# First-half token sums beside the second sample group's cross-attention, three units in the late tail, and low parts of the sums on VectorE

## The chip, the cores and the metric

The kernel runs on one core of a Trainium2 chip, as one program and one launch. The metric is device time in microseconds (us); the time of a kernel is the median of its runs.

## What is computed

One decoder layer for a prompt of 1024 tokens and for 8 sample sequences of 8 tokens, in float32, model width 1024. The change lies between cross-attention and the feed-forward block:

```python
x = x + rmsnorm(mixed, p['g_mix_post'])
x = x + rmsnorm(cross_attend(rmsnorm(x, p['g_ca_pre']), mk, mv, p), p['g_ca_post'])
y, buf_new = conv_ffn(rmsnorm(x, p['g_ffn_pre']), p, buf)

def cross_attend(h, mk, mv, p):
    q = (h @ p['w_cq']).reshape(n, t, CA_HEADS, CA_DH)
    s = jnp.einsum('nthd,nmhd->nhtm', q, mk) * (CA_DH ** -0.5)
    o = jnp.einsum('nhtm,nmhd->nthd', jax.nn.softmax(s, axis=-1), mv)
    return o.reshape(n, t, CA_HEADS * CA_DH) @ p['w_co']

def conv_ffn(h, p, buf):
    u = h @ p['w_up']
    ...
```

The prompt rows attend into one memory of 256 tokens that is computed in the kernel. Each of the 8 sample sequences has its own cached memory keys and values, 2 MB per sequence, read from HBM.

## The kernel before, in words

Every float32 operand is held as a high and a low part (`fp32r`), and one product is three matmuls (`mm3`): high by high, high by low, low by high. TensorE (PE) is the engine on which nearly all depends. VectorE (DVE), ScalarE (ACT) and GpSimd (POOL) make the parts: ACT casts the high part, DVE or POOL subtracts it from the source for the low one. The prompt is worked in two halves of 512 tokens, `actA[0]` and `actA[1]`, each with 8 column blocks of 128. The code is written as Python generators that `weave` interleaves by weight; a scheduler then fixes the final order on each engine, and each engine runs its instructions strictly in that order. SyncE (SP) issues all the DMAs, also in order.

The work around the change, as the generators name it:

- `cross(1)`: cross-attention of the second half of the prompt; scores from `ca_k` (memory keys), a softmax on DVE and ACT, and products with `ca_v` (memory values) into `actA[1]`.
- `cross_sample()`: cross-attention of the samples, in two groups of four sequences (`gq` 0 and 1), 17 steps each. A group has four rounds of keys: four tiles of 256 KB are loaded, transposed on PE (L1431), copied out of PSUM by DVE and ACT, and multiplied into the scores (L1436). Its buffers are eight half rows of 512: four take the loaded tiles and four the transposed ones, so a round's loads wait until the transposes of the round before have read them. Then come one softmax, a transpose (L1444), four rounds of value tiles (16 loads, products L1456), a mask, products L1464, and a split into `hSx`, the sample rows of the next projection.
- `project_rows(wco, ...)`: the output projection of cross-attention, for the first half (with `residual`) and for the second (with `late_rows`). A half is two column halves `n`, each of four weight units `u` (512 KB of weights, split into a ring of three slots); a unit is 24 matmuls of 512 columns on four PSUM banks `j`, one bank for each 128 tokens, and in the second half four more matmuls for the samples (`rows_s`, L1187 and L1188).
- After a half of the projection the rows are normalised, added to the residual (its rows are loaded from `xd`), normalised again with the next gain (L1238 and L321 in the first half; L1627 and L1633, tile by tile, in the second), and turned on PE (L329) into the column form that the up projection reads. In the second half, the last two units of `n` = 1 are done bank after bank (`tail`), so that the rows of bank 0 can start while banks 1 to 3 are still being filled.
- `sums(half, j, ...)`: the up projection is a Strassen-Winograd product, so it needs sums of token quarters. For each of two token tiles of a half, DVE adds and subtracts 128x512 blocks (L1573), and `split` casts four results on ACT (L1558) and subtracts on POOL (L1559) into `T1`, `T2`, `T4` and a quarter of `acts`. `early_sums` is the first half's, `late_tile` the second's.
- Then the up projection runs through 22 column groups of `w_up`. Group 0 is done in two passes, EARLY (first half's tokens, 256 columns) and LATE; from group 1 on the products have 512 columns.

Before the change the order in the code is: the first half's projection woven with `cross(1)` and the whole second sample group; then the second half's projection woven with `early_sums`; then the tail, `late_rows` and group 0.

Of the kernel before, what the change touches and what calls it, by code (L numbers as in the profile page):

```python
# [115 lines left out]
def tile_decoder_step(ctx, tc, cf, x_prompt, x_sample, cache_sb_k, cache_sb_v, state_hgrn,  # L116
# [228 lines left out]

    def wunit(loads, dims):

        i = ring[0] % NRING
        ring[0] += 1
        raw, lo, hi = raw_slot(dims), at(wlr[i], dims, dt=F32R), at(whr[i], dims, dt=F32R)  # L350
# [18 lines left out]

    def unit512(w, k0, c0):  # L370
        return wunit(lambda raw: [(raw, w[k0 * 128:(k0 + 2) * 128, c0:c0 + 512].rearrange("(k p) n -> p k n", p=128))], [2, 512])

# [797 lines left out]

    def project_rows(w, ah, al, hs, done, nk=8, unit=None, last=False, order=(4, 0, 1, 2, 3)):

        for n in range(2):
            pj = [dtile() for _ in range(4)]
            pS = smp() if hs is not None else None

# [6 lines left out]

            def rows_s(u, wh, wl):
                for kk in range(2):
                    k = 2 * u + kk
                    PE.matmul(pS, hs[:, k, :], wh[:, kk, :], start=k == 0, stop=False)  # L1187
                    PE.matmul(pS, hs[:, k, :], wl[:, kk, :], start=False, stop=k == nk - 1)  # L1188

            tail = 2 if last and n == 1 else 0  # L1190
            for u in range(nk // 2 - tail):
                ww = unit512(w, 2 * u, n * 512)
                for j in range(4):
                    rows(j, u, *ww)
                    if j == 1:
                        yield
                if hs is not None:
# [306 lines left out]

    close_x(3)
    close_x(1, "right")
# [41 lines left out]
    s3t = new(fc, [512])  # L1548
    SP.dma_start(out=vb[:, 0, :], in_=conv_w[0, 0:2].rearrange("j (m c) -> (j m) c", c=128))
    SP.dma_start(out=vb[0:44, 1, :], in_=conv_w[0, 2].rearrange("(m c) -> m c", c=128))  # L1550
    SP.dma_start(out=vb[44:88, 1, :], in_=conv_b[0].rearrange("(m c) -> m c", c=128))
    tpv = aux()
    for j in range(2):
        PE.transpose(out=tpv[:, j * 88:(j + 1) * 88], in_=vb[:, j, :], identity=ident[:88, :88])
    V.tensor_copy(out=cw.rearrange("p j m -> p (j m)"), in_=tpv[:, :176])

    def split(src, dst, eng=G):
# [3 lines left out]

    def sums(half, j, x12, x22):


        cols = slice(j * 128, (j + 1) * 128)
        late = slice(256 + j * 128, 256 + (j + 1) * 128)
        tcol = slice(half * 256 + j * 128, half * 256 + (j + 1) * 128)
        b11, b21 = [[f32(acts[:, half, l, k:k + 4, cols]) for l in range(2)] for k in (0, 4)]
        t3 = [acts[:, half, l, 0:4, late] for l in range(2)]
# [17 lines left out]
        acc(V, ta, ta, b11[1])  # L1587
        split(ta, t3)
        acc(V, tb, b21[0], tb)
        acc(V, tb, tb, b21[1], ALU.add)  # L1590
        split(tb, t4)
        yield

    def early_sums():
        for j in range(2):
            late = slice(256 + j * 128, 256 + (j + 1) * 128)
            yield from sums(0, j, *[[f32(acts[:, 0, l, k:k + 4, late]) for l in range(2)] for k in (0, 4)])

    def late_tile(j):
        if j < 2:  # L1600
            return prompt_dst(*actA[1], j * 128)
# [13 lines left out]
    def late_rows():  # L1615
# [21 lines left out]
        def done(j, n, p):  # L1637
# [12 lines left out]
            if n == 1:  # L1650
                xt = xrb()[:P]
                SP.dma_start(out=xt, in_=xd[i] if i < 8 else xsd)
                return steps(P, y, xt, i, ssc, late_tile(j) if j < 4 else sample_dst(hSf))
        return done
# [538 lines left out]
```

## Time and profile before

| what | value |
|---|---|
| runs shown | 1978.38, 1985.63, 1988.15 us; median 1985.63 |
| profiled execution, its own time | 1981.71 us |
| its span | 1979.9 us |
| PE busy | 1847.7 us, 93% |
| DVE busy | 1479.0 us, 75% |
| ACT busy | 918.6 us, 46% |
| POOL busy | 674.5 us, 34% |

Busy time is the time in which an engine has an instruction; the span runs from the first instruction to the last, and some 1.8 us of the execution's own time lie outside it. Times inside the execution are counted from the span's start.

### The profile page before, as it was taken

What the parts mean: (1) busy time and instruction counts of PE and PEld (TensorE: products, weight loads), DVE (VectorE), ACT (ScalarE), POOL (GpSimd) and SP (SyncE); (2) the same over time, 40 slices, a digit from 0 to 9 for tenths busy, and PEclk for the clock granted to TensorE, in tenths of its full rate; (3) what the DMA queues carried; (4) which work ended last, traced back from release to release, by engine and by line L of the source; (5) the groups of instructions that cost most, each with busy time, mean ns of one, the idle gap of its engine ahead of it and who ended that gap; (6) DMA issues with size and microseconds to landing.
All of it is one profiled execution on the core that took longest, in us unless ns stands there. A gap on an engine that the chain in (4) does not pass through costs nothing. (4 is left out here: it accounts for less than half of the span.)

```text
span 1979.9 us, 28696 instructions
## 1 busy us (share of the span) xinstructions
PE 1847.7 (93%) x10270; PEld 1493.8 (75%) x10270; DVE 1479.0 (75%) x2343; ACT 918.6 (46%) x1726; POOL 674.5 (34%) x552
## 2 busy tenths in 40 slices
PE   7998999998999899999899996899999999999897
PEld 6777877876887566777787775788888888887775
DVE  6587686678658675665655479889899899878695
ACT  6554364364346443344444345444444444544443
POOL 3102202202201322000400014655655655556884
PEclk9999899999899999999999998899999999999998
DMA  6211211111112655564226643222223333474531
GB/s 196 60 40 39 63 35 49 51 46 57 45 62 71 193 187 179 158 226 146 62 85 198 199 139 107 63 80 80 81 88 101 106 98 101 161 282 140 190 129 48
DMA packets 185388, 219.84 MB, mean 111 GB/s; under 512 B 24962, under 2 KB 116502, under 8 KB 184918
## 3 DMA queue, kind: packets, MB, share of 16 engines
q1 hardware_dynamic: 185246, 218.01, 34.9%
q8 instruction: 81, 1.33, 0.3%
q14 instruction: 61, 0.50, 0.1%
HBM read 171.19 MB, written 47.13 MB: 110 GB/s over the span
## 5 line engine op out<-in xcount | busy, mean ns | idle before, releaser
L374 PE MATMUL d<-act,arena_r 128*128 128x512 f32 (+1 forms) x640 | 257.4, 402 | 8.0 <-DVE arena_f L1692 6.3
L375 PE MATMUL d<-act,arena_r 128*128 128x512 f32 (+1 forms) x640 | 253.4, 396 | 0.0
L376 PE MATMUL d<-act,arena_r 128*128 128x512 f32 (+1 forms) x640 | 252.9, 396 | 0.3 <-DVE arena_r L1559 0.3
L374 PE MATMUL d<-arena_r,act 128*128 128x512 f32 (+1 forms) x576 | 205.1, 358 | 0.1
L375 PE MATMUL d<-arena_r,act 128*128 128x512 f32 (+1 forms) x576 | 202.4, 351 | 0.9 <-DVE arena_r L354 0.8
L376 PE MATMUL d<-arena_r,act 128*128 128x512 f32 (+1 forms) x576 | 202.7, 352 | 0.0
L1559 POOL TENSOR_TENSOR ffn_s<-arena_f,ffn_s 128x512 fp32r<-128x512 f32 x87 | 153.0, 1768 | 132.1 <-ACT ffn_s L1558 132.1
L1729 DVE SCALAR_TENSOR_TENSOR arena_f<-arena_f 128x64 f32<-128x64 f32 (+2 forms) x176 | 189.2, 1105 | 2.4 <-ACT arena_f L1727 1.4
L354 POOL TENSOR_TENSOR arena_r<-arena_f,arena_r 128x1024 fp32r<-128x1024 f32 (+1 forms) x34 | 81.3, 2398 | 266.5 <-ACT arena_r L353 230.4
L374 PEld LDWEIGHTS d<-act,arena_r 128*128 128x128 f32 x640 | 122.5, 191 | 33.1 <-DVE arena_f L1692 6.5
L353 ACT CAST arena_r<-arena_f 128x1024 fp32r<-128x1024 f32 (+1 forms) x96 | 98.6, 1028 | 98.9 <-PE d L376 21.7
L376 PEld LDWEIGHTS d<-act,arena_r 128*128 128x128 f32 x640 | 121.6, 190 | 26.9 <-DVE arena_r L1559 0.5
L375 PEld LDWEIGHTS d<-act,arena_r 128*128 128x128 f32 x640 | 122.0, 191 | 23.2
L1692 DVE TENSOR_TENSOR arena_f<-d,arena_f 128x512 f32<-128x512 f32 (+1 forms) x173 | 111.8, 661 | 25.6 <-PE d L376 21.6
L374 PEld LDWEIGHTS d<-arena_r,act 128*128 128x128 f32 x576 | 110.2, 192 | 20.7 <-issue 6.9
L354 DVE TENSOR_TENSOR arena_r<-arena_f,arena_r 128x1024 fp32r<-128x1024 f32 (+1 forms) x62 | 74.5, 1203 | 66.5 <-ACT arena_r L353 66.5
L375 PEld LDWEIGHTS d<-arena_r,act 128*128 128x128 f32 x576 | 110.1, 191 | 17.1 <-DVE arena_r L354 2.1
L376 PEld LDWEIGHTS d<-arena_r,act 128*128 128x128 f32 x576 | 110.1, 191 | 15.2 <-issue 2.5
L1559 POOL TENSOR_TENSOR arena_r<-arena_f,arena_r 128x1024 fp32r<-128x1024 f32 (+1 forms) x44 | 106.1, 2428 | 23.9 <-ACT arena_r L1558 23.8
L1727 ACT ACTIVATE arena_f<-arena_f 128x64 f32<-128x64 f32 (+1 forms) x88 | 69.4, 836 | 45.1 <-DVE arena_f L1692 44.9
L1559 POOL TENSOR_TENSOR ffn_T<-ffn_f,ffn_T 128x512 fp32r<-128x512 f32 x12 | 20.1, 1678 | 189.7 <-ACT ffn_T L1558 189.7
L1679 DVE TENSOR_TENSOR arena_f<-arena_f 128x512 f32<-128x512 f32 x84 | 78.3, 933 | 4.2 <-POOL ffn_s L1559 3.5
(580 smaller groups left out, 4964.4 us busy)
## 6 DMA issues: line engine op xcount, KB each, us to landing
arena_f<-in_w_up_dram SPq DMA_DIRECT2D x88, 256.0 KB, 3.1
arena_f<-in_w_in_dram SPq DMA_DIRECT2D x52, 256.0 KB, 3.4
gd<-arena_f SPq DMA_DIRECT2D x22, 512.0 KB, 2.6
arena_f<-in_w_o_dram SPq DMA_DIRECT2D x16, 512.0 KB, 4.1
arena_f<-in_w_cq_dram SPq DMA_DIRECT2D x16, 512.0 KB, 3.8
arena_f<-in_cache_mem_k_dram SPq DMA_DIRECT2D x32, 256.0 KB, 3.4
arena_f<-in_w_co_dram SPq DMA_DIRECT2D x16, 512.0 KB, 3.9
arena_f<-in_cache_mem_v_dram SPq DMA_DIRECT2D x32, 256.0 KB, 4.1
```

The costliest lines, as they stand in the source:

```text
L353: newest[0] = S.copy(out=hi, in_=raw)
L354: lo_engine().tensor_tensor(out=lo, in0=raw, in1=f32(hi), op=ALU.subtract)
L374: PE.matmul(p, ah, bh, start=first, stop=False)
L375: PE.matmul(p, ah, bl, start=False, stop=False)
L376: PE.matmul(p, al, bh, start=False, stop=last)
L1559: eng.tensor_tensor(out=dst[1], in0=src, in1=f32(dst[0]), op=ALU.subtract)
L1679: eng.tensor_tensor(out=o, in0=a, in1=b, op=op)
L1692: V.tensor_tensor(out=out, in0=a, in1=b, op=ALU.add)
L1727: S.activation(out=c, in_=taps[2], func=AF.Identity, scale=cw[:, 2, m:m + 1], bias=cw[:, 3, m:m + 1])
L1729: V.scalar_tensor_tensor(out=outs[i], in0=taps[i], scalar=cw[:, i, m:m + 1], in1=outs[i], op0=ALU.mult, op1=ALU.add)
```

## The change

Five edits.

1. The second sample group leaves the stretch of the first half's projection. That projection's last nine steps are woven with `cross(1)` alone; its rows go through new buffers (`rows`) where `ca_v` lay; and only when its norms have been issued are the 17 steps of the group woven with `early_sums` and the first three steps of the second half's projection.
2. In the second half's projection the sample rows of column half 0 run one unit behind (`behind_`), because `hSx` is not there yet.
3. The tail of the second half's projection takes three units for each bank instead of two; the third has its own place in `ffn_s`.
4. The late tiles keep a full float32 copy of the first two transposed tiles (`whole`, an extra ACT copy out of PSUM), so that each of the second half's sums needs one operand where it needed two.
5. All `split`s of `sums` subtract on DVE instead of POOL.

```diff
-    def wunit(loads, dims):
+    def wunit(loads, dims, place=None):
...
-    def project_rows(w, ah, al, hs, done, nk=8, unit=None, last=False, order=(4, 0, 1, 2, 3)):
+    def project_rows(w, ah, al, hs, done, nk=8, unit=None, last=None, order=(4, 0, 1, 2, 3)):
...
-            pS = smp() if hs is not None else None
+            pS = None
+            behind_ = []
...
-            tail = 2 if last and n == 1 else 0
+            tail = len(last) if last and n == 1 else 0
...
                 if hs is not None:
-                    rows_s(u, *ww)
+                    behind_.append((u, *ww))
+                    if len(behind_) > (last is not None and n == 0):
+                        rows_s(*behind_.pop(0))
                 yield
+            for x in behind_:
+                rows_s(*x)
             if tail:
...
-                wws = [unit512(w, 2 * u, n * 512) for u in us]
+                wws = [unit512(w, 2 * u, n * 512, place) for u, place in zip(us, last)]
...
-    xtr, xnr = Rot(cr.bufs[:2]), Rot(cr.bufs[2:])
-    yr = Rot([])
+    xtr, xnr, yr = Rot([]), Rot([]), Rot([])
...
-    weave((late[0], 11), (late[1], 17), (late[2], 8))
+    weave((late[0], 11), (itertools.islice(late[2], 9), 9))
     close_x(3)
+    open_x("rows", XO + 4096, 4096, F32)
+    xtr.bufs, xnr.bufs = ([at(XO + 4096 + D * (2 * i + j), [D]) for j in range(2)] for i in range(2))
+    for _ in late[2]:
+        pass
+    close_x()
...
-    def sums(half, j, x12, x22):
+    def sums(half, j, b11, b21, x12, x22):
...
-        acc(V, ta, ta, b11[1])
+        for x in b11[1:]:
+            acc(V, ta, ta, x)
...
-        split(tb, t2)
-        split(ta, t1)
+        split(tb, t2, V)
+        split(ta, t1, V)
...
-        split(tb, t4)
+        split(tb, t4, V)
...
+            whole[j] = y3 = y.rearrange("p (c t) -> p c t", t=128)
+            def dst(c0, n, tp):
+                split_(c0, n, tp)
+                S.copy(out=y3[:, c0:c0 + n, :], in_=tp)
...
-                run_.append(sums(1, j - 2, [tp], x22))
+                run_.append(sums(1, j - 2, [whole[j - 2][:, 0:4]], [whole[j - 2][:, 4:8]], [tp], x22))
...
-    last = project_rows(wco, *actA[1], hSx, late_rows(), last=True, order=(0, 1, 2, 3, 4))
-    weave((itertools.islice(last, 14), 14), (early_sums(), 4))
+    last = project_rows(wco, *actA[1], hSx, late_rows(), last=[(SOFF, SOFF + 1024), None, None], order=(0, 1, 2, 3, 4))
+    weave((late[1], 17), (early_sums(), 4), (itertools.islice(last, 3), 3))
...
+    for _ in itertools.islice(last, 9):
+        pass
     raws = up_load(0)
```

What this makes of the engines' order is seen at three places. In the changed program the same lines have other numbers: L376 to L378 are the `mm3` lines L374 to L376, L1442, L1447, L1455, L1467 and L1475 are the sample group's L1431, L1436, L1444, L1456 and L1464, and L1194 and L1195 are the sample rows' L1187 and L1188.

The first place is PE in the second sample group. Before, the group's transposes and scores stand between matmuls of the first half's projection (`d`) and scores of `cross(1)` (`aux<-ca_k,act`):

```order
L1436 MATMUL smp<-arena_f 32x128 x16
L1431 MATMUL aux<-arena_f 128x128 x4
L374 MATMUL d<-arena_r,act 128x512
L375 MATMUL d<-arena_r,act 128x512
L1431 MATMUL aux<-arena_f 128x128 x12
L374 MATMUL aux<-ca_k,act 128x256
```

In the changed program PE has, from the first half's row transposes (L329) on, these rows in one piece up to the first sample rows (L1194):

```order
L378 MATMUL d<-arena_r,act 128x512
L329 MATMUL aux<-arena_f,rows 128x128 x20
L1442 MATMUL aux<-arena_f 128x128 x16
L1447 MATMUL smp<-arena_f 32x128 x2
L1442 MATMUL aux<-arena_f 128x128 x4
L1447 MATMUL smp<-arena_f 32x128 x14
L1442 MATMUL aux<-arena_f 128x128 x8
```

and, at the end of that piece:

```order
L1442 MATMUL aux<-arena_f 128x128 x12
L1447 MATMUL smp<-arena_f 32x128 x16
L1455 MATMUL aux<-arena_f 128x128 x2
L1467 MATMUL smp<-arena_f 32x512 x8
L1475 MATMUL aux<-arena_f 128x32 x4
L1763 MATMUL aux<-arena_f 128x88 x2
L1467 MATMUL smp<-arena_f 32x512 x8
L1475 MATMUL aux<-arena_f 128x32 x4
L1194 MATMUL smp<-arena_r 128x512
```

No matmul of a projection stands in the group any more. Three units of the second half's projection (72 matmuls) stand ahead of it: 65 before the first row transpose, 7 between the transposes. The fourth unit needs the ring slot of the first, which is free only after the sample rows L1194 and L1195.

The second place is ACT where the late rows begin: `L311 ACTIVATE arena_f,st<-d` is the sum of squares of late bank 0. Before, the casts of the first half's last sums (`ffn_T`, `act`) stand in front of it:

```order
L1558 CAST ffn_T_10080<-ffn_f 128x4x128
L1558 CAST ffn_T_10088<-ffn_f 128x4x128
L1558 CAST arena_r<-arena_f 128x1024
L1558 CAST act<-ffn_f 128x4x128
L1558 CAST ffn_T_10084<-ffn_f 128x4x128
L311 ACTIVATE arena_f,st<-d 128x512
```

In the changed program there are only casts of weights in front of it:

```order
L311 ACTIVATE arena_f,sS<-arena_f 64x512
L355 CAST arena_r<-arena_f 128x1024
L1566 CAST arena_r<-arena_f 128x1024
L311 ACTIVATE arena_f,st<-d 128x512
L298 ACTIVATE rs_t<-ssum,arena_f 128x1
```

The early sums have moved ahead, into the second sample group.

The third place is DVE in the late rows, where the third bank's transposed tile is summed. Before, between two norms (L1633 on full rows, L1627 on the samples' 64):

```order
L1633 SCALAR_TENSOR_TENSOR arena_f<-arena_f,rs_y 128x1024
L1573 TENSOR_TENSOR ffn_f<-aux,ffn_f 128x512
L1627 SCALAR_TENSOR_TENSOR arena_f<-arena_f,rs_y 64x1024
L1573 TENSOR_TENSOR ffn_f<-ffn_f,act 128x512
L1559 TENSOR_TENSOR act<-aux,act 128x4x128
```

In the changed program (L1645 is the line L1627, L1651 is L1633, L1579 is L1573, L1567 is L1559):

```order
L1567 TENSOR_TENSOR ffn_T_9850<-ffn_f,ffn_T_9850 128x4x128
L1645 SCALAR_TENSOR_TENSOR arena_f<-arena_f,rs_y 64x1024
L1651 SCALAR_TENSOR_TENSOR arena_f<-arena_f,rs_y 128x1024
L1567 TENSOR_TENSOR ffn_T_9858<-ffn_f,ffn_T_9858 128x4x128
L1579 TENSOR_TENSOR ffn_f<-ffn_f,arena_f 128x512
L1567 TENSOR_TENSOR act<-aux,act 128x4x128
```

The low parts (`ffn_T`) now stand in DVE's own queue; fewer sums stand beside them.

## Rows read from the trace of the kernel before

**Rows 1.** Windows: us, busy time of PE, PEld, DVE, ACT, POOL (instructions), granted clock, DMA.
```profile
1086.00:1138.00 52.00, 52.00 (x407) 39.50 (x406) 25.62 (x58) 19.45 (x43) 0.00 (x0) 1.00 0.61 204
1198.00:1250.00 52.00, 30.96 (x184) 28.27 (x184) 48.35 (x93) 26.44 (x63) 24.26 (x17) 0.77 0.28 92
```

**Rows 2.** Who PE waited for, 1086 to 1257 us, nine rows: total, times, longest.
```profile
PE aux L329 <- DVE arena_f L1633: 9.2, 2, 8.3
...
PE d L376 <- DVE arena_r L1559: 0.3, 1, 0.3
```

**Rows 3.** ACT in order of time: start, duration, instruction, idle before it and releaser.
```profile
1196.29 0.62 ACT L1558 CAST ffn_T<-ffn_f 128x512 fp32r<-128x512 f32 x1 [3.89 <-DVE ffn_f L1573]
1196.93 0.60 ACT L311 ACTIVATE arena_f<-d 128x512 bf16<-128x512 f32 x1
```

**Rows 4.** PE in order of time, pieces.
```profile
1086.19 2.04 PE L1431 MATMUL aux<-arena_f 128*128 128x128 f32 x16
...
1156.12 0.39 PE L374 MATMUL d<-arena_r,act 128*128 128x512 f32 x1
...
1157.29 0.40 PE L376 MATMUL d<-arena_r,act 128*128 128x512 f32 x1
1159.57 1.09 PE L329 MATMUL aux<-arena_f 128*128 128x128 f32 x8 [1.89 <-DVE arena_f L321]
...
1205.77 1.97 PE L329 MATMUL aux<-arena_f 128*128 128x128 f32 x8 [8.34 <-DVE arena_f L1633]
...
1256.64 0.28 PE L376 MATMUL d<-act,arena_r 128*128 128x256 f32 x1
1256.76 0.39 PE L374 MATMUL d<-act,arena_r 128*128 128x512 f32 x1
```

**Rows 5.** The first half's norms: ACT and DVE in order of time, pieces.
```profile
1140.48 0.60 ACT L311 ACTIVATE arena_f<-d 128x512 bf16<-128x512 f32 x1 [0.71 <-PE d L376]
...
1143.86 2.48 DVE L1238 SCALAR_TENSOR_TENSOR ca_y<-ca_y,rs_y,arena_f 128x1024 f32<-128x1024 f32 x2
...
1158.23 3.75 DVE L321 SCALAR_TENSOR_TENSOR arena_f<-ca_y,rs_y,arena_f 128x1024 f32<-128x1024 f32 x3
```

**Rows 6.** PE by lines, 1086 to 1138 us, the sample group's five: busy us, mean ns.
```profile
L1431 PE MATMUL aux<-arena_f 128*128 128x128 f32 x64 | 8.3, 275 | 0.0
...
L1444 PE MATMUL aux<-arena_f 128*128 128x128 f32 x2 | 0.4, 286 | 0.0
```

**Rows 7.** By tile: `xd`, memory keys, then memory values with their issues' durations (ns).
```profile
DMA to landing us min/median/max: 3.5/3.9/4.3
...
DMA to landing us min/median/max: 2.6/3.2/5.6
...
L1453 SPq DMA_DIRECT2D arena_f<-in_cache_mem_v_dram x16: 328/382/418, 1105.9 to 1122.3; - x16
...
DMA to landing us min/median/max: 3.0/4.2/5.4
```

**Rows 8.** The second group's softmax on DVE, in order of time.
```profile
1111.93 0.42 DVE L1373 TENSOR_REDUCE mx<-smp 128x1 f32<-128x256 f32 x1 [1.88 <-PE smp L1436]
...
1114.38 0.42 DVE L1446 COPY arena_f<-aux 128x256 f32<-128x256 f32 x1 [0.59 <-PE aux L1444]
```

**Rows 9.** DVE by lines, 1197.5 to 1245.4 us: busy us, mean ns, idle before.
```profile
L1627 DVE SCALAR_TENSOR_TENSOR arena_f<-arena_f,rs_y 128x1024 f32<-128x1024 f32 (+1 forms) x5 | 7.8, 1568 | 0.0
L1573 DVE TENSOR_TENSOR ffn_f<-ffn_f,act 128x512 f32<-128x512 f32 x7 | 6.9, 983 | 0.8 <-POOL ffn_T L1559 0.8
L1633 DVE SCALAR_TENSOR_TENSOR arena_f<-arena_f,rs_y 128x1024 f32<-128x1024 f32 (+1 forms) x5 | 6.4, 1273 | 0.0
L302 DVE TENSOR_TENSOR rs_t<-rs_t,rs_m 128x1 f32<-128x1 f32 (+1 forms) x10 | 5.3, 535 | 0.0
...
L1573 DVE TENSOR_TENSOR ffn_f<-aux,ffn_f 128x512 f32<-128x512 f32 x2 | 1.3, 674 | 0.0
...
L300 DVE TENSOR_SCALAR rs_m<-ssum 128x1 f32<-128x1 f32 (+1 forms) x5 | 0.7, 145 | 0.1
```

More of the change, by code (lines that the diff above doesn't have):

```diff
@@ L344, in sample_dst @@
         return dst
-    def wunit(loads, dims):
-        i = ring[0] % NRING
-        ring[0] += 1
-        raw, lo, hi = raw_slot(dims), at(wlr[i], dims, dt=F32R), at(whr[i], dims, dt=F32R)
+    def wunit(loads, dims, place=None):
+        if place is None:
+            i = ring[0] % NRING
+            ring[0] += 1
+            place = wlr[i], whr[i]
+        raw, (lo, hi) = raw_slot(dims), (at(o, dims, dt=F32R) for o in place)
         for view, src in loads(raw):
@@ L368, in units256, with unit512 @@
         return res
-    def unit512(w, k0, c0):
-        return wunit(lambda raw: [(raw, w[k0 * 128:(k0 + 2) * 128, c0:c0 + 512].rearrange("(k p) n -> p k n", p=128))], [2, 512])
+    def unit512(w, k0, c0, place=None):
+        return wunit(lambda raw: [(raw, w[k0 * 128:(k0 + 2) * 128, c0:c0 + 512].rearrange("(k p) n -> p k n", p=128))], [2, 512], place)
     def mm3(p, ah, al, bh, bl, first, last):
@@ L1184, in rows_s @@
             def rows_s(u, wh, wl):
+                nonlocal pS
+                pS = pS or smp()
                 for kk in range(2):
@@ L1548, in tile_decoder_step @@
     s3t = new(fc, [512])
[L1549 to L1555, printed above, removed]
     def split(src, dst, eng=G):
@@ L1560, in split @@
         return dst
-    def sums(half, j, x12, x22):
-        cols = slice(j * 128, (j + 1) * 128)
+    def sums(half, j, b11, b21, x12, x22):
         late = slice(256 + j * 128, 256 + (j + 1) * 128)
         tcol = slice(half * 256 + j * 128, half * 256 + (j + 1) * 128)
-        b11, b21 = [[f32(acts[:, half, l, k:k + 4, cols]) for l in range(2)] for k in (0, 4)]
         t3 = [acts[:, half, l, 0:4, late] for l in range(2)]
@@ L1583, in sums @@
             acc(V, tb, tb, x22[1], ALU.add)
-        split(tb, t2)
-        split(ta, t1)
+        split(tb, t2, V)
+        split(ta, t1, V)
         acc(V, ta, tb, b11[0])
-        acc(V, ta, ta, b11[1])
-        split(ta, t3)
+        for x in b11[1:]:
+            acc(V, ta, ta, x)
+        split(ta, t3, V)
         acc(V, tb, b21[0], tb)
-        acc(V, tb, tb, b21[1], ALU.add)
-        split(tb, t4)
+        for x in b21[1:]:
+            acc(V, tb, tb, x, ALU.add)
+        split(tb, t4, V)
         yield
@@ L1595, in early_sums, with late_tile @@
         for j in range(2):
-            late = slice(256 + j * 128, 256 + (j + 1) * 128)
-            yield from sums(0, j, *[[f32(acts[:, 0, l, k:k + 4, late]) for l in range(2)] for k in (0, 4)])
-    def late_tile(j):
+            cols, late = (slice(o + j * 128, o + (j + 1) * 128) for o in (0, 256))
+            yield from sums(0, j, *[[f32(acts[:, 0, l, k:k + 4, c]) for l in range(2)] for c in (cols, late) for k in (0, 4)])
+    whole = {}
+    def late_tile(j, y):
         if j < 2:
-            return prompt_dst(*actA[1], j * 128)
+            split_ = prompt_dst(*actA[1], j * 128)
+            whole[j] = y3 = y.rearrange("p (c t) -> p c t", t=128)
+            def dst(c0, n, tp):
+                split_(c0, n, tp)
+                S.copy(out=y3[:, c0:c0 + n, :], in_=tp)
+            return dst
         x22 = []
@@ L1652, in done @@
                 SP.dma_start(out=xt, in_=xd[i] if i < 8 else xsd)
-                return steps(P, y, xt, i, ssc, late_tile(j) if j < 4 else sample_dst(hSf))
+                return steps(P, y, xt, i, ssc, late_tile(j, y) if j < 4 else sample_dst(hSf))
         return done
@@ L1736, in tile_decoder_step @@
     NGRP = 22
-    last = project_rows(wco, *actA[1], hSx, late_rows(), last=True, order=(0, 1, 2, 3, 4))
-    weave((itertools.islice(last, 14), 14), (early_sums(), 4))
+    last = project_rows(wco, *actA[1], hSx, late_rows(), last=[(SOFF, SOFF + 1024), None, None], order=(0, 1, 2, 3, 4))
+    weave((late[1], 17), (early_sums(), 4), (itertools.islice(last, 3), 3))
+    SP.dma_start(out=vb[:, 0, :], in_=conv_w[0, 0:2].rearrange("j (m c) -> (j m) c", c=128))
+    SP.dma_start(out=vb[0:44, 1, :], in_=conv_w[0, 2].rearrange("(m c) -> m c", c=128))
+    SP.dma_start(out=vb[44:88, 1, :], in_=conv_b[0].rearrange("(m c) -> m c", c=128))
+    tpv = aux()
+    for j in range(2):
+        PE.transpose(out=tpv[:, j * 88:(j + 1) * 88], in_=vb[:, j, :], identity=ident[:88, :88])
+    V.tensor_copy(out=cw.rearrange("p j m -> p (j m)"), in_=tpv[:, :176])
+    for _ in itertools.islice(last, 9):
+        pass
     raws = up_load(0)
```

## The prediction

> **What bounds the kernel now.** I read the windows first. PE is the engine that nearly everything waits for, and where the second sample group stands today it is busy 52.00 of 52.00 us at a granted clock of 1.00 [rows 1]. So the group, with its loads and its softmax, is hidden there; the reader is to see that nothing was being waited for. The weak place comes later: from 1198 to 1250 us PE is busy 30.96 of 52.00 us, at a mean granted clock of 0.77 (of 2.4 GHz; it moves between 1.2 and 2.4), while DVE is busy 48.35 [rows 1]. Then I read who PE waited for: nine rows from 1086 to 1257 us, of 9.2 down to 0.3 us, 24.3 together, nearly all on DVE's late rows [rows 2]. The longest, 8.34 us [rows 4], has its origin on ACT: late bank 0's sum of squares starts at 1196.93, when banks 1 to 3 are full too (36 matmuls, 8.4 us, after bank 0), because the cast in front of it, of the first half's last sum, waited 3.89 us for DVE [rows 3]. That is what the change goes for.
>
> I work between two points that stand at the same place in both orders: the group's first transposes, at 1086.19 us, and the first 512-column product of the up projection's group 1, at 1256.76 [rows 4]. PE does the same instructions between them before and after, so only what it loses counts. Before, that is 24.3 us of waits and some 8 of half clock: what stands from 1198 to 1250 us takes about 23 us at the rates below, and was busy 30.96 [rows 1]. Together **32.3 us lost before**. Rates at full clock: a 512-column matmul 0.234 us (five steps from 1156.12 to 1157.29), a 256-column one 0.12, eight transposes about 1.0, from 1.09 with its overlap [rows 4].
>
> **What the change loses, part by part.**
>
> *Cross-attention of the prompt without the group between it* (edit 1). PE's order has fewer other matmuls between scores and their transposes, about 2.6 us where the softmax needs 2 when undisturbed (1111.93 to 1114.38, with a transpose in it) [rows 8]. I take 1 us, between 0 and 2.
>
> *The first half's norms.* From the last bank's sum of squares, 1140.48, to the first row transpose, 1159.57, take 19.1 us [rows 4, 5]. In the changed order PE has 12 products with `ca_v` and 65 matmuls to cover them: 77 by 0.234 is 18.0 us. But the residual's rows are now loaded to where `ca_v` lay, so the load waits for those 12 products (2.8 us) and lands 3.9 later [rows 7]: with 0.3 for the issue, 7.0 us after the last bank, where the first use stood at 3.4 (1143.86) [rows 5]. That is 3.6 late, and the wait is 19.1 + 3.6 − 18.0 = 4.7. Then the transposes: DVE has three norms (3.75 us [rows 5]), six subtractions of 0.68 and a norm of 1.27 [rows 9] before the last tile, 9.1 us; PE starts after the first norm and ends 1.0 after the last, 8.9 us, with 32 transposes (3.8) and 7 matmuls (1.6) to do: 3.5 lost. Before, the sample rows and the units stood between them. Together 8.2; low end 4.6 (load on time), high 10.
>
> *The second sample group, alone on PE.* Its own work is 20.0 us as the five rows have it [rows 6], 18 from start to start. Its length now: the first four tiles, 2.4. Three rounds of reloads: a tile's load is issued when its buffer has been transposed, lands after 2.6 to 5.6 us, median 3.2 [rows 7]; a round ends with the last of four issued together, so I take 4.2, with 0.15 to issue and 0.45 for four transposes 4.8, three times 14.4. Copy and last scores 1.7. Softmax to the copied transpose: 2.9 us undisturbed [rows 8], and five early sums of 0.67 that now stand between its steps on DVE: 6.0, since a small part hides behind the exponential. Two rounds of values that are there, 2.0. Two more that can only be loaded when those are read: eight issues of 0.38, the last landing up to 5.4 later [rows 7], 8.7, of which 1.0 is covered: 7.7. Last products, mask, L1464 and split, 3.4. Sum 37.6, of which PE works 18: **19.6 lost**. No projection matmul can fill this: the three units stand ahead of the row transposes, and the fourth's ring slot is freed behind the group. If they did stand inside it, the 17 us taken from here would be missing under the norms, so that would be worth nearly nothing. Low end: every load lands in 2.6 us and no sum disturbs, 28.1 long, 10.1 lost. High end: 45 long, 27 lost. The early sums (26 instructions of 0.67, 17.5 us of DVE) are hidden in it. On SP the group's loads now stand behind the first half's loads of `xd` and its four stores, which are issued before the group can use a tile; behind the last value loads stand the residual rows and the tail's weights, whose first use is some 15 us later. Both cost nothing as long as that holds.
>
> A rule bears on the loads. The Trainium skill ("DMA: Bandwidth & Descriptors", Anatomy of one DMA) gives a transfer about 2 us and then its bytes at 436 GB/s; a tile of 256 KB would take an estimated 2.6 us. The trace agrees for the fastest load alone (2.6); its medians and maxima are above it, and the measurement decides. By the page the group would be about 28 us long and the sum some 9.5 lower.
>
> *Behind the group.* The fourth unit's high and low part can only be made after the samples' matmuls of the first: 1 us (0 to 4, if the clock is low here).
>
> *The late rows* (edits 3 to 5, and the early sums gone from in front). Bank 0's chain now starts when the bank is full. From there to the sample rows' split, which the up projection's L1700 needs, DVE's queue holds, by the order: 4 products with the gain by 0.69, 5 row splits by 0.68, 10 norms by 1.27, the samples' gain 1.3, a weight split 1.2, the samples' fold 0.7, one evacuation 0.4, some 45 small ones by 0.145 to 0.18, and of the second half's sums 7 additions and 8 subtractions by 0.67 (before: 12 and 5 evacuations; so edits 4 and 5 nearly cancel on DVE) [rows 9]. Together 40.3, and 0.7 for the first sum of squares. POOL disturbs it: three rows are 7.6 us above what their clean forms take (L302 0.535 for 0.145, L1627 1.568 for 1.273, L1573 0.983 for 0.674 [rows 9]), with 17 POOL instructions in that time [rows 1], 0.45 each; edit 5 leaves some eight: 3.6. The four extra copies of edit 4 (0.6 each) are on ACT, which is busy 26.44 of 52 us there [rows 1]; I take nothing for them, 2 us if they stood in the chain. So 44.6 us (before: 48.4, from 1196.93 to 1245.3). In it PE has 54 matmuls of the tail (12.6), 12 of the samples (2.8), 48 early products (5.8) and 40 transposes (4.9): 26.1. Lost: **18.5** (14.9 without POOL, 22.5 with all 7.6).
>
> **Sum.** 1 + 8.2 + 19.6 + 1 + 18.5 = 48.3 us lost, against 32.3: 16.0 us more. On the profiled execution's own 1981.7 (span 1979.9) that makes 1997.7, so **1998 us**; from group 1 on PE is the bound and passes the delay on. The median shown, 1985.6, is 3.9 above the profiled one; the range takes that in. With all low ends 29.6 are lost, 1979.0; with all high ends 65.5, 2014.9.
>
> **Rivals.**
>
> *Loads as quick as the fastest.* With one tile in flight behind the other, and no weights beside them, each lands 2.6 us after issue: the group is 28.1 us long, 1988.2. For it: the minimum; the group has the queue nearly to itself. Against: the median of a value load is 4.2. This is the page's rule above. Chance 0.18.
>
> *The late rows stop being waited for* (not slower). If DVE came to the sample rows' split within the 26.1 us of PE's work, 18.5 would go: 1979.2, a little under before. It decides the sign when that stretch falls below 28.6 us. For it: the chain starts at once and has 5 us more of PE under it. Against: DVE's own durations add to 40.3, and DVE is in order. Chance 0.05.
>
> *The clock falls in the group.* From 1198 to 1250, with PE busy 60%, the clock was 0.77, and eight transposes after the 8.34 us wait took 1.97 instead of 1.09 [rows 1, 4]. With the group at 1.2 GHz the PE steps on its path double (three rounds' transposes 1.5, scores 1.0, values and L1464 3.9), and the units behind it start slowly (2): 8.4 more, 2006. For it: PE works 18 of 37.6 us there. Against: it is not idle for long at once. Chance 0.17. [...]
>
> That the change does not do what it says is decided by the order for one part: the three units are not beside the group. The rest does.
>
> **How the numbers follow.** The sum's own case, 1990 to 2004, has 0.55, and 0.05 is left for what I do not see. About 0.5%, 10 us, is what a measurement of this kernel can tell from no change. Slower by more: nearly all of the main case and the low clock, 0.67. Within: quick loads, hidden late rows and the main case's lower edge, 0.28. Faster: 0.05. The range leaves out the two ends' last tenth each, 1983 to 2010.
>
> **What would show it.** Right: in the changed profile PE waits for L1442 on memory-key loads and for L1467 on memory-value loads, some 20 us in all between the first half's row transposes and the samples' L1194; no wait of 8 us in front of the late rows, but 15 to 20 us of waits on DVE behind the tail; group 1's first 512-column product near 1272 us. Wrong: a group of under 30 us, or late rows in which PE is busy throughout.

## The result, and the profile after

The changed kernel takes **1997.5 us** (median; 1991.4 to 2005.3) against 1985.6 for the kernel before (1978.4 to 1990.7, the same number of runs). The ratio is **1.0063, 95% interval 1.0040 to 1.0086**: 12.5 us slower. 1998 was forecast, within 1983 to 2010. The profiled execution took 1995.78 us, span 1993.6, 13.7 over the span of before.

First the windows of the changed kernel (columns as in [rows 1]): the stretch where the second sample group stood, the group in its new place, and the tail.

```profile
1086.00:1138.00 52.00, 52.00 (x262) 43.34 (x261) 28.46 (x62) 23.39 (x54) 0.00 (x0) 1.00 0.31 99
1152.00:1191.00 39.00, 28.98 (x248) 16.09 (x246) 25.86 (x45) 11.29 (x21) 0.00 (x0) 0.91 0.65 208
1222.00:1260.00 38.00, 22.28 (x126) 19.34 (x125) 34.05 (x68) 21.12 (x49) 11.37 (x7) 0.71 0.31 95
```

Where the group used to stand PE is as full as before, 52.00 of 52.00 us, with 262 instructions in place of 407 [rows 1]: the group gave PE nothing to wait for there, and taking it out saves there no more than its own work, which PE has to do elsewhere. Its new stretch is 39 us long. Now PE in order of time, the pieces that answer to [rows 4]: the two points (at 1092.37 and 1275.29), the row transposes, and the second half of the group.

```profile
1092.37 0.39 PE L376 MATMUL aux<-ca_p,ca_v 128*128 128x512 f32 x1
...
1143.72 1.06 PE L329 MATMUL aux<-arena_f,rows 128*128 128x128 f32 x8 [1.73 <-DVE rows L321]
...
1151.37 1.12 PE L329 MATMUL aux<-arena_f,rows 128*128 128x128 f32 x8 [2.75 <-DVE rows L321]
1152.29 1.06 PE L1442 MATMUL aux<-arena_f 128*128 128x128 f32 x4
...
1170.73 1.06 PE L1447 MATMUL smp<-arena_f 128*32 128x128 f32 x26 [0.38 <-ACT arena_f L1443]
1175.21 0.44 PE L1455 MATMUL aux<-arena_f 128*128 128x128 f32 x2 [3.42 <-DVE arena_f L1389]
1176.79 3.27 PE L1467 MATMUL smp<-arena_f 128*32 128x512 f32 x16 [1.14 <-issue]
1180.94 1.08 PE L1475 MATMUL aux<-arena_f 128*128 128x32 f32 x8 [0.89 <-DVE arena_f L1470]
...
1182.14 2.17 PE L1467 MATMUL smp<-arena_f 128*32 128x512 f32 x6
1184.79 3.68 PE L1467 MATMUL smp<-arena_f 128*32 128x512 f32 x10 [0.48 <-DMA arena_f<-in_cache_mem_v_dram]
1189.25 1.08 PE L1475 MATMUL aux<-arena_f 128*128 128x32 f32 x8 [0.79 <-DVE arena_f L1470]
1191.25 0.50 PE L1194 MATMUL smp<-arena_r 128*128 128x512 f32 x1 [0.92 <-DVE arena_r L334]
...
1235.35 1.06 PE L329 MATMUL aux<-arena_f 128*128 128x128 f32 x8 [2.16 <-DVE ssum L1641]
1241.54 1.94 PE L329 MATMUL aux<-arena_f 128*128 128x128 f32 x8 [5.12 <-DVE arena_f L1651]
1249.89 0.58 PE L376 MATMUL d<-ffn_T,ffn_s 128*128 128x256 f32 x1 [6.42 <-ACT ffn_s L1566]
...
1256.20 0.58 PE L1718 MATMUL smp<-arena_r 128*128 128x256 f32 x1 [1.40 <-DVE arena_r L334]
...
1275.29 0.39 PE L376 MATMUL d<-act,arena_r 128*128 128x512 f32 x1
```

From point to point it is 182.9 us, before 170.6 [rows 4]: **12.3 more**, where 16.0 were forecast. The other 1.4 us of the spans' difference lie outside. The first point itself comes 6.2 us later, though PE's instructions up to it are the same; in the profiles of this study it lies anywhere from 1085.0 to 1093.8, so that is no effect of the change. And behind the second point the changed kernel gains 4.8 back, 2.8 of them in group 1, of which 1.5 is one wait: PE waited 3.4 us there before for DVE's fold of the samples' rows and now waits 1.9.

The sequence to note is in the group: the last scores end at 1171.79, the softmax takes until 1175.21, the first values start at 1176.79 and take 3.27 us for 16 matmuls; the next 16 take from 1182.14 to 1188.47. Only 0.48 us of that is put down to a load. The rest of the load wait stands on the weight loader's rows, as the waits of PEld from 1152 to 1191.5 us show (total, times, longest):

```profile
PEld smp L1467 <- DMA arena_f<-in_cache_mem_v_dram: 4.2, 6, 1.4
PEld aux L1475 <- DVE arena_f L1470: 3.9, 2, 2.2
```

while PE's own list from 1092 to 1275.5 us has these for the late rows, the row norms, the softmax and the key loads:

```profile
PE d L376 <- ACT ffn_s L1566: 6.4, 1, 6.4
PE aux L329 <- DVE arena_f L1651: 5.1, 1, 5.1
PE aux L329 <- DVE rows L321: 4.5, 2, 2.8
PE aux L1455 <- DVE arena_f L1389: 3.4, 1, 3.4
...
PE aux L1442 <- DMA arena_f<-in_cache_mem_k_dram: 1.6, 5, 0.5
```

The 8.34 us wait of before [rows 4] is gone. ACT takes bank 0's sum of squares 0.1 us after the bank is full (PE's last product of it ends at 1211.67):

```profile
1211.76 0.60 ACT L311 ACTIVATE arena_f<-d 128x512 bf16<-128x512 f32 x1 [3.41 <-PE d L378]
```

### The profile page after: what moved, and what is told of

The parts are those of the page before. It is cut to its first block, busy times and chain, and to the rows that moved or that the text cites. A ratio compares the mean times of both kernels' runs of the same rounds, so it can differ in the third digit from the quotient of the medians.

```text
span 1993.6 us, 28684 instructions
## 1 busy us (share of the span) xinstructions
PE 1854.5 (93%) x10270; PEld 1493.2 (75%) x10270; DVE 1466.9 (74%) x2353; ACT 923.0 (46%) x1730; POOL 650.4 (33%) x536
## 5 line engine op out<-in xcount | busy, mean ns | idle before, releaser
L376 PE MATMUL d<-act,arena_r 128*128 128x512 f32 (+1 forms) x640 | 255.9, 400 | 1.6 <-ACT arena_r L355 1.6
L378 PE MATMUL d<-act,arena_r 128*128 128x512 f32 (+1 forms) x640 | 252.3, 395 | 0.0
L376 PE MATMUL d<-arena_r,act 128*128 128x512 f32 (+1 forms) x568 | 201.5, 358 | 0.1
L377 PE MATMUL d<-arena_r,act 128*128 128x512 f32 (+1 forms) x568 | 199.3, 351 | 1.0 <-DVE arena_r L356 1.0
L378 PE MATMUL d<-arena_r,act 128*128 128x512 f32 (+1 forms) x568 | 200.0, 352 | 0.0
L1567 POOL TENSOR_TENSOR ffn_s<-arena_f,ffn_s 128x512 fp32r<-128x512 f32 x87 | 153.3, 1770 | 131.9 <-ACT ffn_s L1566 131.2
L1567 POOL TENSOR_TENSOR arena_r<-arena_f,arena_r 128x1024 fp32r<-128x1024 f32 (+1 forms) x44 | 104.9, 2402 | 229.2 <-ACT arena_r L1566 227.7
L376 PEld LDWEIGHTS d<-act,arena_r 128*128 128x128 f32 x640 | 121.3, 190 | 26.3 <-ACT arena_r L355 2.1
L378 PEld LDWEIGHTS d<-act,arena_r 128*128 128x128 f32 x640 | 120.7, 189 | 26.1 <-POOL arena_r L356 0.3
L376 PEld LDWEIGHTS d<-arena_r,act 128*128 128x128 f32 x568 | 108.9, 192 | 17.9 <-issue 4.8
L378 PEld LDWEIGHTS d<-arena_r,act 128*128 128x128 f32 x568 | 108.9, 192 | 15.0 <-issue 2.5
L1697 DVE TENSOR_TENSOR arena_f<-arena_f 128x512 f32<-128x512 f32 x84 | 78.2, 932 | 3.0 <-POOL ffn_s L1567 2.3
L736 POOL TENSOR_TENSOR arena_f<-arena_f 128x256 f32<-128x256 f32 (+1 forms) x41 | 37.4, 917 | 122.4 <-ACT arena_f L735 122.4
```

The costliest lines, as they stand in the source:

```text
L376: PE.matmul(p, ah, bh, start=first, stop=False)
L377: PE.matmul(p, ah, bl, start=False, stop=False)
L378: PE.matmul(p, al, bh, start=False, stop=last)
L736: G.tensor_tensor(out=e4[:, :, 1, :], in0=e4[:, :, 1, :], in1=q4[:, :, 1, :], op=ALU.mult)
L1567: eng.tensor_tensor(out=dst[1], in0=src, in1=f32(dst[0]), op=ALU.subtract)
L1697: eng.tensor_tensor(out=o, in0=a, in1=b, op=op)
```

## The experiments

Two theories were put against each other. **Mine:** edit 1 leaves the group bare on PE and costs some 20 us; edits 3 to 5 earn part of that back in the late rows. **The rival:** the later edits cost something or earn nothing. "Ratio" is to the kernel before, with its 95% interval.

**e1_group_back.** Edit 1 undone, the rest kept (with the samples' products no longer a unit behind, and the sums woven over 12 steps, since a tail of three leaves 12):

```
+    xtr, xnr = Rot(cr.bufs[:2]), Rot(cr.bufs[2:])
...
+    weave((late[0], 11), (late[1], 17), (late[2], 8))
...
-    weave((late[1], 17), (early_sums(), 4), (itertools.islice(last, 3), 3))
+    weave((itertools.islice(last, 12), 12), (early_sums(), 4))
```

> Edit 1 undone: the second sample group stands again among the first half's projection, the early sums again among the last projection's units; the tail of three units, the whole late quarters and the subtractions on VectorE stay. Theory (the changed kernel pays for the group alone on TensorE, some 20 us, and earns back in the late rows): no bare group, no waits for L1442 on loads; bank 0 of the tail is full 18 + 4 matmuls (some 5 us) sooner than in the kernel before, its chain takes 44.6 us and some 4 to 8 us more where early sums still stand in front of it: some 18 to 22 us lost between the two points in place of 32, so 1972 to 1976 us, ratio to before about 0.994. Rival (the three later edits are what costs, or earn nothing): 1985 to 1995 us, ratio 1.000 to 1.005.

Measured: 1974.8 us, ratio 0.9949 (0.9932 to 0.9967), as forecast. So edit 1 (with edit 2, which only serves it) costs 1.0063 − 0.9949 = 1.14%, some 22.6 us, and edits 3 to 5 earn 10.1. Its windows have PE full again where the group stands, with 409 instructions, and the two points are 165.2 us apart (1090.47 to 1255.65). That is 17.7 less than in the changed kernel: so much of edit 1's cost stands in this stretch of the profiled executions, and the 22.6 of the ratios is uncertain by some 6 us, as their intervals have it. It is 5.4 less than before, with 26.9 us lost where I had forecast 18 to 22; another 2.9 of what edits 3 to 5 earn lies behind the second point.

```profile
1086.00:1138.00 52.00, 52.00 (x409) 39.51 (x408) 26.88 (x62) 20.29 (x47) 0.00 (x0) 1.00 0.61 195
```

**e2_sums_behind and e5_sums_out.** The first half's sums are woven among the last projection's units, behind the group. In the first the scheduler moved them back beside the group, so its order is the changed kernel's but for a few rows, and it does not test its forecast. In the second their scratch rows are those that the last value tiles are read from, so that they can't start sooner:

```
-        ta, tb = tts
+        ta, tb = tts if half else [cr.bufs[3][:, 512 * i:512 * (i + 1)].rearrange("p (k t) -> p k t", t=128) for i in range(2)]
```

> As changed, but the first half's token sums are woven among the last projection's units behind the group, not beside the group. Theory: the group gets its softmax back (the 3.4 us wait of its transposes shrinks to about 1), but 26 instructions of 0.67 us (17.5 us) now stand on VectorE in the 20 us ahead of the tail, so that bank 0's chain starts 3 to 8 us late: 1995 to 2002 us, level with the changed kernel's 1997.5. Rival (the sums beside it are what makes the group long): group under 33 us long, 1990 us or less.

> As changed, but the first half's token sums use other scratch rows, which the group's last value tiles are read from, so that all 26 instructions stand behind the group's values on VectorE (in e2_sums_behind the scheduler had moved them into the group again, so that run was a repeat of the changed kernel). Theory: inside the group about 3 us come back (softmax to the copied transpose from 5.3 us towards 3), and the chain of the late rows starts late, since 17.5 us of sums, 3.6 of weight splits and 2.8 of products with the gain stand on VectorE in the 20 us ahead of bank 0: 3 to 8 us lost: 1997 to 2004 us. Rival (the sums cost nothing behind the group, where TensorE has its projection): 1990 to 1994 us.

Measured: 1995.9 us, ratio 1.0062 (1.0042 to 1.0081), a repeat of the changed kernel; and 1999.7, ratio 1.0091 (1.0072 to 1.0110), inside the band of the theory. Between the two points the repeat took 184.5 us, 1.6 more than the changed kernel, which tells how far two profiled executions of one order differ. The sums beside the group cost little there. With them out, the group is 38.4 us long in place of 39.0, and the wait for the softmax 2.04 in place of 3.42 (PE in order of time, e5_sums_out):

```profile
1172.34 0.65 PE L1455 MATMUL aux<-arena_f 128*128 128x128 f32 x2 [2.04 <-DVE arena_f L1389]
1173.56 1.08 PE L1467 MATMUL smp<-arena_f 128*32 128x512 f32 x4 [0.56 <-issue]
```

Behind the group they hold up the late rows: DVE turns to bank 0 at 1214.71, 124.2 us behind the first point (1090.55 here), where it was 120.1 in the changed kernel, and the last subtraction ahead of it took 2.49 us after a wait for ACT (DVE in order of time, e5_sums_out):

```profile
1212.30 2.49 DVE L1567 TENSOR_TENSOR ffn_T<-arena_f,ffn_T 128x512 fp32r<-128x512 f32 x1 [0.69 <-ACT ffn_T L1566]
1214.71 0.68 DVE L1663 TENSOR_TENSOR arena_f<-d,arena_f 128x512 f32<-128x512 f32 x1
```

**e3_splits_pool.** Edit 5 undone on the changed kernel, at all four places:

```
-        split(tb, t2, V)
+        split(tb, t2)
```

> As changed, but the sums' low parts are subtracted on GpSimd again (16 instructions of 128x512). Theory: VectorE loses 8 subtractions of 0.67 us in the late rows (5.4 us) and gains back what 8 more GpSimd instructions disturb (3.6 us by my estimate of 0.45 each) and what VectorE or ScalarE waits for them: within 3 us of the changed kernel, 1994 to 2001 us. Rival (edit 5 is the cost): 1991 us or less. Rival (edit 5 is the gain): 2003 us or more.

Measured: 2002.9 us, ratio 1.0094 (1.0070 to 1.0118). Its median is 5.4 us over the changed kernel's, above my "level" (1994 to 2001) and next to the second rival's band (the edit is the gain). The two ratios' intervals overlap, so this run alone does not settle it; between the two points it takes 189.6 us against 182.9 and 184.5 (e2), and e8 below finds the same gain clear of noise. PE now waits 3.9 us for POOL itself, 0.6 in the changed kernel, and 8.3 for ScalarE's casts in front of those subtractions, where it was 6.4 (waits of PE from 1090 to 1280 us):

```profile
PE d L376 <- ACT ffn_s L1566: 8.3, 2, 6.2
...
PE d L378 <- POOL ffn_s L1567: 3.9, 2, 2.2
```

**e4_no_reloads.** The group without 20 of its 32 loads:

```
-                    for s4, kt_ in enumerate(kts):
+                    for s4, kt_ in enumerate(kts if gq == 0 or mcx + c0 == 0 else []):
...
-                    for s4, vt_ in enumerate(vts):
+                    for s4, vt_ in enumerate(vts if gq + n < 2 else []):
```

> As changed, but the second sample group loads only its first four key tiles and its first eight value tiles; the other 12 key tiles and 8 value tiles are not loaded, and the tiles already there are used in their place (this part of the output is therefore not the reference's). Theory (loads are the largest part of the group's length beyond TensorE's own work): key rounds 3 to 5 us shorter, second pair of value rounds about 6 us shorter: group 39 to some 29 us, 1985 to 1990 us. Rival (the waits that the trace puts down to loads, 3.3 us, are all there is, the rest is VectorE with sums between): 1993 to 1996 us.

Measured: 1991.1 us, ratio 1.0029 (1.0012 to 1.0045): 6.4 us less than the changed kernel, between the two bands; the group shrank less than the theory's 10 us. It is 31.1 us long, 7.9 less (1148.88 to 1179.96). PE in order of time shows where it gained, and what stayed without any load to wait for:

```profile
1165.56 1.07 PE L1447 MATMUL smp<-arena_f 128*32 128x128 f32 x28 [0.58 <-DVE arena_f L1443]
1169.64 0.41 PE L1455 MATMUL aux<-arena_f 128*128 128x128 f32 x2 [3.01 <-DVE arena_f L1389]
1170.61 3.57 PE L1467 MATMUL smp<-arena_f 128*32 128x512 f32 x16 [0.56 <-issue]
1175.07 1.92 PE L1467 MATMUL smp<-arena_f 128*32 128x512 f32 x16 [0.89 <-DVE arena_f L1470]
...
1179.96 0.50 PE L1194 MATMUL smp<-arena_r 128*128 128x512 f32 x1 [0.92 <-DVE arena_r L334]
```

The second 16 values take 1.92 us, where they took 6.3 with loads. The four key rounds take 17.7 us (to 1166.62), where they took 19.5: only 1.8 of their length was loads. In these 17.7 us PE shows only 1.8 of idle time; but from the start of a transpose to the start of the next instruction 0.17 us pass on average, where it was 0.11 in the kernel before, among the projection's matmuls.

**Edits 3 to 5 apart.** Four more kernels in which group and early sums stand as in the kernel before: e6_tail_two has edits 4 and 5, e7_no_whole 3 and 5 (with the `late_tile` of before), e8_before_splits_dve 5 alone, and e11_tail_three_alone 3 alone. The lines that differ, first e6 and e7 from e1_group_back, then e8 from the kernel before (four such lines), then e11 from e7:

```
-    last = project_rows(wco, *actA[1], hSx, late_rows(), last=[(SOFF, SOFF + 1024), None, None], order=(0, 1, 2, 3, 4))
-    weave((itertools.islice(last, 12), 12), (early_sums(), 4))
+    last = project_rows(wco, *actA[1], hSx, late_rows(), last=[None, None], order=(0, 1, 2, 3, 4))
+    weave((itertools.islice(last, 14), 14), (early_sums(), 4))
...
-                run_.append(sums(1, j - 2, [whole[j - 2][:, 0:4]], [whole[j - 2][:, 4:8]], [tp], x22))
+                run_.append(sums(1, j - 2, *[[f32(acts[:, 1, l, k:k + 4, (j - 2) * 128:(j - 1) * 128]) for l in range(2)] for k in (0, 4)], [tp], x22))
...
-        split(tb, t2)
+        split(tb, t2, V)
...
-        split(tb, t2, V)
+        split(tb, t2)
```

> The kernel of e1_group_back with edit 3 undone: a tail of two units, 14 steps ahead of it. Theory: bank 0 is full some 5 us later and the early sums still end in time, so TensorE has 5 us less to do while it waits for the late rows: 1978 to 1981 us, 4 to 6 over the 1974.8 of e1_group_back. Rival (the sums decide when the late rows can start, so a fuller tail gives nothing): 1973 to 1976 us.

> The kernel of e1_group_back with edit 4 undone: the late sums read high and low parts of the first two late tiles, with 12 additions where 8 stand now, and the four extra copies on ScalarE are gone. Theory: four VectorE instructions more of 0.67 us in the late chain, 2.7 us: 1976 to 1979 us. Rival (the ScalarE copies stand in the chain and cost as much): 1973 to 1975.5 us.

> The kernel before with edit 5 alone: the sums' low parts on VectorE, 16 subtractions moved there. Theory (that edit gives most of what the later edits earn, as in e3_splits_pool, where undoing it cost 5.4 us): 1978 to 1981 us, ratio 0.997. Rival (it helps only with a tail of three, since early sums on VectorE grow by 5.4 us in front of bank 0): 1985 to 1989 us.

> The kernel before with edit 3 alone: a tail of three units, the group and the early sums where they were, their low parts subtracted on GpSimd. Theory: edits 3 and 5 work on the same wait. With the early sums' end held up by GpSimd and ScalarE (the 3.89 us in front of bank 0's sum of squares), an earlier bank 0 helps little: 1981 to 1985 us, ratio 0.999 to 1.000. Rival (the two add up: 0.9944 against 0.9967 says 0.23% for edit 3): 1978 to 1981 us.

```
edits   kernel                 us      ratio   95% interval      between the points, us
none    the kernel before                                        170.6
3 4 5   e1_group_back          1974.8  0.9949  0.9932 to 0.9967  165.2
  4 5   e6_tail_two            1979.3  0.9988  0.9971 to 1.0006  165.8
3   5   e7_no_whole            1973.5  0.9944  0.9923 to 0.9964  163.2
    5   e8_before_splits_dve   1975.4  0.9967  0.9949 to 0.9984  163.7
3       e11_tail_three_alone   1978.7  0.9971  0.9956 to 0.9986  165.8
```

The kernel before took 1983.4 to 1985.4 us beside these, so the ratios are what to compare. Edit 3 alone is worth 0.29%, edit 5 alone 0.33%, both 0.56%. By the medians they add up, against what I expected of e11, which came out with its rival. But each ratio is known to some 0.2%, and the last column (one profiled execution each) does not bear it out: there edit 3 alone saves 4.8 us, edit 5 alone 6.9, and both only 7.4. Whether they add up stays open; that each helps alone is clear of noise. Edit 4 gives nothing that can be measured (0.9949 against 0.9944, 0.9988 against 0.9967, intervals overlapping), so e7 came out with its rival too; e6 and, by its ratio, e8 came as forecast. **Edits 3 and 5 without edit 1 have the lowest median found: 1973.5 us, faster than both kernels**, though no interval separates them from e1_group_back or from edit 5 alone.

**e9_samples_first and e10_samples_third.** The best version with the sample rows' tail ahead of bank 0 (e9) or between banks 1 and 2 (e10, where the line ends in `order=(0, 1, 4, 2, 3))`):

```
-    last = project_rows(wco, *actA[1], hSx, late_rows(), last=[(SOFF, SOFF + 1024), None, None], order=(0, 1, 2, 3, 4))
+    last = project_rows(wco, *actA[1], hSx, late_rows(), last=[(SOFF, SOFF + 1024), None, None], order=(4, 0, 1, 2, 3))
```

> The kernel of e7_no_whole (group and early sums as in the kernel before, tail of three, subtractions on VectorE) with the sample rows' tail first, ahead of bank 0. Theory: VectorE's in-order queue sets the end of the late rows, its work is the same, and only what stands last in it changes: the samples' 16 matmuls (2 us) leave the path and up to 2 us of late products with them, while bank 0 is full 2.8 us later: 1970 to 1974 us, within 4 us of e7_no_whole (1973.5). Rival (the delay of bank 0's chain goes through in full): 1975 to 1978 us.

> The kernel of e7_no_whole with the sample rows' tail between banks 1 and 2. Theory: bank 0's chain starts as early as in e7_no_whole, the samples' norm no longer stands behind the late sums on VectorE: 1970 to 1973 us. Rival (the sums of the last two banks are then last and the late products wait for them): 1974 to 1977 us.

Measured: 1974.7 us, ratio 0.9954 (0.9932 to 0.9975), level with e7_no_whole and between its two bands; and 1983.4, ratio 0.9997 (0.9980 to 1.0014), worse than both its bands. In e10 PE waits less for the late rows' norms (3.1 us; 6.2 in e7_no_whole), but 10.9 us for the samples' fold of the up projection (waits of PE from 1160 to 1290 us, e10_samples_third):

```profile
PE aux L1725 <- DVE arena_f L383: 10.9, 2, 6.0
PE aux L329 <- DVE arena_f L1645: 3.1, 2, 2.1
```

That fold stands on DVE behind the sums of the last two banks (DVE in order of time, without a gap, e10_samples_third); in e7_no_whole the same wait is 1.6 us. Neither order beats it.

```profile
1237.90 0.69 DVE L1582 TENSOR_TENSOR ffn_f<-ffn_f,act 128x512 f32<-128x512 f32 x1
1238.50 0.69 DVE L1582 TENSOR_TENSOR ffn_f<-aux,act 128x512 f32<-128x512 f32 x1
1239.10 0.41 DVE L383 TENSOR_TENSOR arena_f<-smp,arena_f 64x256 f32<-64x256 f32 x1
```

## Why the prediction was right, and which of its terms were off

The step that decided it holds: the second sample group was hidden before, and is bare now. Undoing it (e1) takes 22.6 us off by the ratios, 17.7 between the two points. That 1998 lies so near to 1997.5 is luck: the sum was 3.7 us too high between the points, and the profiled execution that it was added to lies 3.9 below the median shown. By the prediction's own terms, in its order:

- **Lost before, 32.3 us.** Not tested apart. It stands behind the next line.
- **Lost after, 48.3 forecast.** PE's work between the points is 170.6 − 32.3 = 138.3 us; 182.9 leaves 44.6 lost.
- **Cross-attention without the group, 1 us.** It lost nothing: PE is full to 1138 us.
- **The first half's norms, 8.2 us.** Measured 4.5 (1.73 and 2.75). This term carries most of the 3.7 us by which the sum is off. The loads into `rows` did wait for `ca_v`, and DVE first used one 6.5 us after the last bank's sum of squares (from 1124.16 to 1130.69; 7.0 forecast). But I added those 3.6 us to a chain of 19.1 read off the kernel before, and here the chain to the first row transposes, at 1143.72, took 19.6 in all: a late start was not passed on in full. In the kernel before, DVE had also waited for later loads of `xd` in that chain (0.56 and 1.43 us), and two splits of weights stood in it (1.23 each) that do not stand there now (ACT, then DVE in order of time, changed kernel).

```profile
1124.16 0.60 ACT L311 ACTIVATE arena_f<-d 128x512 bf16<-128x512 f32 x1 [0.72 <-PE d L378]
...
1130.69 2.48 DVE L1249 SCALAR_TENSOR_TENSOR ca_y<-ca_y,rs_y,rows 128x1024 f32<-128x1024 f32 x2 [1.98 <-DMA rows<-xd]
```

- **The group, 37.6 us long, 19.6 lost.** Measured 39.0 long, so 21.0 lost. The size was right and the make-up was not. I had the key rounds wait for loads, 4.8 us each. They are nearly as long without any load (17.7 us for four, e4). That transposes, copies out of PSUM and scores there follow each other with nothing else to fill the gaps is my reading; no run tests it. The sums between the softmax's steps cost 1.4 us of its wait (e5), where I had 3. What the loads cost is 7.9 us of the group, most of it at the second pair of value tiles (7.7 forecast for that pair; 8.4 from 1180.06 to 1188.47, and 2.8 for the same pieces in e4).
- **The fourth unit, 1 us.** No wait of over 0.1 us shows on PE between the samples' first product, at 1191.25, and the tail.
- **The late rows, 44.6 us from bank 0 full to the sample rows' split.** Measured 44.5 (1211.67 to about 1256.1). That the total fits to 0.1 us is luck in part. DVE was busy for 38.57 us of the stretch, less than the 40.3 and 3.6 of the sum, because I added up whole durations where an instruction of 0.68 us starts 0.60 behind the last; and it was idle for some 5 us in between, mostly waiting for ACT's results, which the sum had at nothing. Two parts are borne out: edit 4 nearly cancels (e1 against e7), and POOL's instructions disturb DVE. The small L302 takes 0.26 us on average here, before 0.54 [rows 9]; the one that runs beside POOL's L1697 takes 1.21, the others 0.14 to 0.16. The price that I gave edit 5 was too small: its loss is 5.4 us in the medians (e3), where I expected it to be level. Windows, then DVE by lines and in order of time, then POOL, changed kernel:

```profile
1211.67:1256.10 44.43, 28.86 (x154) 24.24 (x153) 38.57 (x84) 25.37 (x63) 8.19 (x5) 0.79 0.27 90
...
L302 DVE TENSOR_TENSOR rs_t<-rs_t,rs_m 128x1 f32<-128x1 f32 (+1 forms) x10 | 2.5, 259 | 0.1
...
1247.99 1.21 DVE L302 TENSOR_TENSOR rs_t<-rs_t,rs_m 64x1 f32<-64x1 f32 x1
...
1247.47 1.71 POOL L1697 TENSOR_TENSOR arena_f<-arena_f 128x512 f32<-128x512 f32 x1
```

**The rivals.** *Loads as quick as the fastest* did not come: the fastest load of keys landed after 2.7 us, of values after 3.6 (first keys, then values, all 32 issues each, of both groups). Its group of 28.1 us was also added up wrongly: in the prediction's terms loads of 2.6 us take 4.8 off the key rounds and 2.8 off the last pair, which leaves 30.0, or 26.9 with an undisturbed softmax. Without 20 of the loads the group is 31.1 (e4). The landing times lie above the Trainium skill's figure for a transfer of this size ("DMA: Bandwidth & Descriptors", Anatomy of one DMA), an estimated 2.6 us. That section measured transfers issued by GpSimd, and these are issued by SyncE; the measurement decides:

```profile
DMA to landing us min/median/max: 2.7/3.5/4.3
...
DMA to landing us min/median/max: 3.6/4.3/5.2
```

*The late rows no longer waited for* did not come either: PE still loses some 18 of the 44.5 us, if its work there is the 26.1 of the prediction (not tested). *The clock falls in the group* came in part. After the 2.75 us wait and after the softmax the granted clock was 0.58 on average (of 2.4 GHz, so mostly at 1.2), and 1.00 in the later key rounds and from the first values' end on (windows, changed kernel):

```profile
1152.30:1156.30 4.00, 3.42 (x20) 2.66 (x18) 3.52 (x6) 1.40 (x3) 0.00 (x0) 0.58 0.26 79
...
1164.00:1168.00 4.00, 3.61 (x50) 2.58 (x49) 3.39 (x6) 1.69 (x3) 0.00 (x0) 1.00 0.80 243
...
1176.70:1180.10 3.40, 3.27 (x16) 0.68 (x16) 3.18 (x5) 1.24 (x2) 0.00 (x0) 0.58 0.10 23
...
1182.10:1188.50 6.40, 5.88 (x18) 1.10 (x16) 0.34 (x1) 0.00 (x0) 0.00 (x0) 1.00 0.73 236
```

Its price is small by my estimate: 16 values took 3.27 us there and 1.92 at full clock (e4), 1.35 more; the first 16 key transposes 3.5 without their gap, where 2 × 1.09 is the rate, 1.3 more. Together 2.7 us, not the 8.4 of the rival, because PE came back to 1.00 each time. The load waits of 0.1 to 0.5 us in each key round did not bring the clock down. The Trainium skill's rule ("TensorE: Matmul & The Clock Gate", Loop structure matters more than you think) is about a long wait for DMA between every matmul, so it does not say that these short ones would; the trace agrees with it only in that the clock was lower behind the two long waits, which were not for loads. In the late rows the clock was low before and after: 0.77 from 1198 to 1250 us [rows 1], 0.71 now from 1222 to 1260.

**Of the signs named**, the missing 8 us wait, the late waits on DVE (2.2, 5.1, 1.4, and 6.4 for ACT) and the late group 1 (1275.3, of which 6.2 from ahead of the first point; 1272 forecast) came. Of these, 8.7 us are put down to DVE and 6.4 to ACT, so the 15 to 20 us on DVE came only with ACT's share. The 20 us of waits for loads did not: PE and PEld together name 6.6 us.

**Open:** how much of the group's remaining 31 us is the order of its steps, and how much its few buffers. A version with more load buffers was not run, nor one with matmuls of a projection among the group's in its new place.

## What to carry to other kernels

- Work that is hidden under a full engine costs nothing there, so moving it frees nothing there; ask what will cover it in the new place. Here PE was busy for 52.00 of 52.00 us in the old place with the group and without it; in the new one some 18 us of work took 39.0.
- A bundle of edits should be priced one by one: here one cost 1.1%, two earned 0.6% together, and one did nothing that could be measured. The two alone have the lowest median.
- A chain of small dependent steps on an engine that stands alone can be long even when no data is late: 31.1 us here without 20 of 32 loads, for some 18 us of PE's work. Don't read its length off the loads alone; look at its turns between engines too.

## What was not expected of the hardware

- A load wait can hide in busy time: 16 matmuls that take 1.92 us were shown over 6.3 us, with 5.88 of the window "busy" and 0.48 of idle time, and the wait itself on the weight loader's rows (4.2 us).
- Sixteen subtractions of 128x512 on VectorE in place of GpSimd made the kernel 0.33% faster (e8), 6.5 us, although VectorE was the busier of the two (75% against 34%) and each takes it 0.67 us.
